# Six inverse roots spread over the partitions by a row in DRAM, windowed attention in another order, and the first loads in smaller pieces

## The chip, the cores and the metric

The kernel runs as one program on one core of one Trainium2 chip. Its engines are TensorE (PE, matrix products into PSUM), VectorE (DVE), ScalarE (ACT), GpSimd (POOL) and SyncE (SP, which issues the DMAs here). Each engine works through its own instructions in program order and waits for the others by semaphores. The metric is the device time of one execution in microseconds (us), the median of three runs.

## The reference

Two blocks over 512 tokens of width 1024, in fp32, one after the other. Cut to the shape of the work (`h` is a normed input, every `@` a product with a weight matrix from DRAM):

```python
def first_block(x, p, ...):
    q, k, v, z_a, b, c, u, z_c = split(rms_norm(x, g) @ w_in, 8)      # 512 columns each
    attn = diff_attention(q, k, v, lam, slopes)                        # 4 heads, two softmaxes each, causal by chunks
    attn = rms_norm(attn, subln_gain, 1e-5) * (1 - lambda_init) * silu(z_a)
    conv = b * causal_conv3(c * u) * silu(z_c)
    x = x + rms_norm(concat(attn, conv) @ w_out, g)
    e = rms_norm(p @ w_ple_proj, g)
    return x + sigmoid(x @ w_ple_gate) * e

def second_block(h, ...):
    u, v, z = split(rms_norm(h, g) @ a_w_in, 3)                        # 2048 columns each
    s = causal_spatial_mix(layer_norm(gelu(v)), w_s, b_s)              # within 128 tokens
    h = h + rms_norm((gelu(u) * s * silu(z)) @ a_w_out, g)
    k, v = split(rms_norm(h, g) @ w_kv, 2)
    q, z = split(rms_norm(h, g) @ b_w_in, 2)
    o = sliding_window_attention(q, k, v, sinks)                       # 16 heads, 4 key heads, window 128
    return h + rms_norm((o * silu(z)) @ b_w_out, g)
```

An `rms_norm` multiplies by `(mean(x^2) + eps)^-0.5` for each token. The kernel does the product with the weight matrix on the un-normed input and multiplies by this inverse root behind it, so that the product need not wait for the norm.

## The kernel before

**Tiles.** Activations lie feature by feature: a tile holds 128 features by 512 tokens. Each fp32 operand is split in two fp32r parts, high and low, and a product is three matmuls (high by high, high by low, low by high). Weights stream from DRAM in tiles `raw` of 128x1024 (512 KB), three in flight. ACT copies a half of one to the high part `whi`, DVE subtracts to get the low part `wlo` (`wsplit`); `wload` issues the DMAs on SP. A `raw` buffer is free once the second `wlo` has read it, and only then the next `raw` can be issued.

**Stages, in the order of time.** `w_in` (6 to 212 us) with the four heads of the first attention between its matmuls; `w_out` (to 255), `w_ple` (to 268) and the gate (to 313); `a_w_in` with the spatial mix (to 593); `a_w_out` (to 682); keys and values (to 706); `b_w_in` (to 831) with the windowed attention between its matmuls, the last of it between those of `b_w_out` (to 886); then the last norm and the output.

**Order.** Every part of the work outside the big products is a generator. A planner (`Flow`) keeps a modelled clock of each engine and resumes a generator when the modelled time of what it waits for has come on TensorE's clock, or, at `yield n`, n modelled ns later. So the program's order on all engines is fixed by these modelled times; `PACE_H`, `H_START` and the like are such delays. The engines themselves know nothing of it and just wait for what is late.

**Norms.** A norm's per-token sums (`st`, eight narrow matmuls) give `var` on DVE and `rstd = var^-0.5` on POOL, as a tile of 128 tokens x 4. To multiply features by it, each partition needs the same row of 512 tokens, the tile `n1rb` (norm n1, of the input), `anrb` (one for each head of the first attention) or `n4rb` (the norm ahead of `a_w_in`). `bcast_wide` makes it for these six and for two others: DVE splits `rstd` into `rh` and `rl`, POOL writes two 128x512 tiles `dgh` and `dgl` with these on the diagonals, and TensorE multiplies both by a matrix of ones (two `bc` matmuls). ACT copies the sum out of PSUM. Each helper records its operations under its own line: `tt` L211, `act` L202, `stt` L207, `ts` L220, `ptt` L215, `dma` L239, `mm` L244, `transpose` L254.

**Names.** First attention: `sc` scores, `s` weights (DVE combines two softmaxes by `rs`, the inverse sums), `tr` their transposes on PE, `pth`/`ptl` their parts, `pv` the product with v, `at` the normed head (DVE, L207). `ev`, `za`: products of `w_in` columns with `n1rb` on DVE. Spatial mix: `rs` at PE are row sums of the masked `w_s`, issued at the end of `spatial_weights`. Windowed attention: a unit is (pair of key heads, query block, which of the two heads), 16 in all; `swa_master` starts them in the order of `ORDER_B`. A unit makes scores `bsc`, weights `be`, transposes `btr`, their parts `bph`/`bpl`, and `bpv`; when both units of a (pair, block) are done, DVE makes `y`, ACT `ybh` and DVE `ybl`, the parts that `b_w_out` reads. `b_w_out` takes blocks 0 and 1 of both pairs first, then blocks 2 and 3. `h_tokens` transposes the residual (`ht`, four transposes a time, eight times) for the last sum.

Of the kernel before, what the change touches and what calls it, by code (L numbers as in the profile page):

```python
# [10 lines left out]
F32 = mybir.dt.float32  # L11
# [6 lines left out]
P = 128  # L18
# [19 lines left out]
ORDER_B = tuple((pr, b) for pr in range(2) for b in range(4))  # L38
AHEAD_END = 1
H_START = 8000  # L40
LAM_AT = 40000
WIDE = ('an', 'n1', 'n3', 'n4', 'n6')
LAT = 130.0
KLATE = 3
BANKS = 7

PACE_A, PACE_B, PACE_LN, PACE_H = 4500, 3500, 8000, 4000
# [106 lines left out]
def block(ctx: ExitStack, tc: tile.TileContext, xT, pT, w_in, w_out, w_ple, w_gate, a_w_in, a_w_out,  # L154
# [7 lines left out]
    whl = ctx.enter_context(tc.tile_pool(name="whl", bufs=WHL))  # L162
    small = ctx.enter_context(tc.tile_pool(name="small", bufs=6))
# [96 lines left out]
    def wsplit(n):  # L260
        raw = raws.pop(n)
        t0 = F.t
        if n in KEPT:
            his, los = [[rt("wk", F32R) for _ in range(2)] for _ in range(2)]
        else:
            hi = whl.tile([P, 1024], F32R, tag="hi", name=nm("whi"))
            lo = whl.tile([P, 1024], F32R, tag="lo", name=nm("wlo"))
            his, los = [[w[:, :512], w[:, 512:]] for w in (hi, lo)]
        for c in range(2):
            r = raw[:, c * 512:(c + 1) * 512]  # L270
            act(his[c], r, AF.Copy, after=t0)
            yield [his[c]]
            if wpos[3] < n:
                yield lambda: wpos[3] >= n
            tt(los[c], r, his[c].bitcast(F32), ALU.subtract, after=t0)

        def part(a, n):

            return his[a // 512][:, a % 512:a % 512 + n], los[a // 512][:, a % 512:a % 512 + n]

        hls[n] = part
        wpos[3] = n + 1
        wload(wpos[2] - 1)

    def wload(cur):
        while wpos[0] < min(len(SEQ), cur + AHEAD_RAW + 1) and wpos[3] >= wpos[0] - WRAW + 1:
# [3 lines left out]
            if wpos[0] < 3:  # L290

                for k in range(2):
                    c = slice(k * 512, k * 512 + 512)
                    dma(nc.sync, raw[:, c], drams[name][i][:, c])
                    dma(nc.sync, x[2 * wpos[0] + k], xT[2 * wpos[0] + k])
# [155 lines left out]

    def norm(stat, d, name, n=1024, eps=EPS, copy=True, half=None):
# [7 lines left out]
        yield [r]  # L460
        if name in WIDE:
# [63 lines left out]
    for k in range(KD):  # L525
# [6 lines left out]
        act(hi, x[k], AF.Copy, scale=v1(V_PRE, k))  # L532
# [169 lines left out]
    def attn_pv(h):  # L702
# [14 lines left out]
        if "an" in WIDE:  # L717
            os = []
            yield from bcast_wide(r, os)
            bc = os[0]  # L720
        else:
            bc = bcast(r)
        rb = rt("anrb")
        act(rb, bc, AF.Copy)
# [222 lines left out]
    def spatial_weights():  # L947
# [18 lines left out]
        yield 4000  # L966
# [410 lines left out]
```

## Time and profile before

| | us |
|---|---|
| median of 3 runs | 894.42 (894.36 to 894.44) |
| profiled execution | 894.61 |
| its span, first to last instruction | 892.9 |
| TensorE busy in the span | 882.8 (99%) |
| VectorE busy | 637.9 (71%) |
| ScalarE busy | 443.4 (50%) |
| GpSimd busy | 77.8 (9%) |
| mean granted clock of TensorE | 0.999 |

The profiled execution stands 0.2 us above the median, and 1.7 us of it lie outside the span. A busy TensorE is not always at its peak: its matmuls are pipelined, and a row's duration is longer than the distance to the next row's start. What a matmul takes of the time is read from the starts of two rows, and a wait from how far a start lies behind the one that the row ahead would allow.

### The profile page before, as it was taken

How to read it: one execution, taken by the hardware profiler on the slowest of the kernel's cores; microseconds unless marked ns; L12 is line 12 of the kernel's file. 1: busy time of each engine (PE TensorE's matmuls, PEld its weight loads, DVE VectorE, ACT ScalarE, POOL GpSimd, SP SyncE). 2: the span in 40 equal slices, each digit the busy share in tenths (PEclk: the TensorE clock that was granted, in tenths of full speed). 3: DMA queues.
4: the chain of work that ended last, by engine and by line, in shares of the span. 5: the costliest groups of instructions: out<-in, count | busy, mean ns of one | idle time of the engine just before them, and what ended most of it. 6: DMA issues, size and time to landing. Idle time of an engine off the chain costs nothing.

```text
span 892.9 us, 12066 instructions
## 1 busy us (share of the span) xinstructions
PE 882.8 (99%) x4348; PEld 744.2 (83%) x4348; DVE 637.9 (71%) x1364; ACT 443.4 (50%) x954; POOL 77.8 (9%) x93
## 2 busy tenths in 40 slices
PE   9999999999999999999999999999999999999997
PEld 7888888888888888888888888888899988887785
DVE  6799989653558893338897766683347876989974
ACT  7455554322556544335443333322344646999763
POOL 0100032100000001001000000000000011434100
PEclk9999999999999999999999999999999999999999
DMA  7231222225423242232232222214232158211353
GB/s 263 94 118 48 71 72 71 95 94 189 142 72 116 73 135 104 99 104 81 73 106 88 89 95 95 95 48 141 94 119 72 71 138 223 65 48 48 120 187 118
DMA packets 30443, 93.20 MB, mean 104 GB/s; under 512 B 3888, under 2 KB 4272, under 8 KB 30384
## 3 DMA queue, kind: packets, MB, share of 16 engines
q1 hardware_dynamic: 30384, 92.44, 30.8%
q8 instruction: 34, 0.56, 0.2%
q14 instruction: 25, 0.20, 0.1%
HBM read 85.60 MB, written 2.10 MB: 98 GB/s over the span
## 4 chain that ended last, share of the span: by engine, by line
PE 87%; DVE 9%; issue 1%; ACT 1%; DMA 1%; SPq 0%; DVEq 0%; ACTq 0%
PE a_w_in L244 29%; PE w_in L244 17%; PE a_w_out L244 10%; PE b_w_in L244 6%; PE w_gate L244 5%; PE w_out L244 5%; PE b_w_out L244 4%; PE kv L244 3%; PE sp L244 2%; DVE wlo L211 2%; PE e L244 1%; PE bsc L244 1%; DVE bpl L211 1%; PE sc L244 1%; DVE be L227 1%
## 5 line engine op out<-in xcount | busy, mean ns | idle before, releaser
L211 DVE TENSOR_TENSOR wlo<-raw,whi 128x512 fp32r<-128x512 f32 x280 | 189.1, 701 | 99.4 <-ACT whi L202 95.6
L202 ACT ACTIVATE whi<-raw 128x512 fp32r<-128x512 f32 x280 | 166.4, 623 | 132.5 <-PE a_w_in L244 39.4
L244 PE MATMUL a_w_in<-h2h,whi 128*128 128x512 f32 x256 | 99.8, 390 | 0.0
L244 PE MATMUL a_w_in<-h2l,whi 128*128 128x512 f32 x256 | 99.7, 390 | 0.0
L244 PE MATMUL a_w_in<-h2h,wlo 128*128 128x512 f32 x256 | 99.6, 389 | 0.0
L244 PE MATMUL w_in<-h1h,whi 128*128 128x512 f32 x224 | 89.3, 401 | 0.4 <-ACT h1h L202 0.4
L244 PE MATMUL w_in<-h1h,wlo 128*128 128x512 f32 x224 | 87.0, 390 | 0.0
L244 PE MATMUL w_in<-h1l,whi 128*128 128x512 f32 x224 | 86.9, 390 | 0.0
L215 POOL TENSOR_TENSOR rstd<-var,mhalf 128x4 f32<-128x4 f32 (+2 forms) x15 | 14.7, 981 | 592.9 <-DVE var L222 536.8
L244 PEld LDWEIGHTS a_w_in<-h2h,wlo 128*128 128x128 f32 x256 | 48.1, 188 | 10.2
L244 PEld LDWEIGHTS a_w_in<-h2h,whi 128*128 128x128 f32 x256 | 48.1, 188 | 9.6
L244 PEld LDWEIGHTS a_w_in<-h2l,whi 128*128 128x128 f32 x256 | 48.1, 188 | 9.4
L211 DVE TENSOR_TENSOR sq<-sq,sq 128x512 f32<-128x512 f32 (+1 forms) x44 | 29.3, 666 | 35.5 <-ACT sq L202 33.6
L244 PE MATMUL b_w_in<-hbh,whi 128*128 128x512 f32 x128 | 52.0, 406 | 0.1
L244 PE MATMUL b_w_in<-hbh,wlo 128*128 128x512 f32 x128 | 50.1, 391 | 0.0
L244 PE MATMUL b_w_in<-hbl,whi 128*128 128x512 f32 x128 | 50.0, 391 | 0.0
L244 PE MATMUL a_w_in<-whi,h2h 128*128 128x512 f32 x128 | 50.0, 391 | 0.0
L244 PE MATMUL a_w_in<-whi,h2l 128*128 128x512 f32 x128 | 49.8, 389 | 0.0
L244 PE MATMUL a_w_in<-wlo,h2h 128*128 128x512 f32 x128 | 49.8, 389 | 0.0
L244 PEld LDWEIGHTS w_in<-h1h,whi 128*128 128x128 f32 x224 | 42.4, 190 | 8.8 <-ACT h1h L202 0.7
L244 PEld LDWEIGHTS w_in<-h1h,wlo 128*128 128x128 f32 x224 | 42.0, 188 | 9.0
L244 PEld LDWEIGHTS w_in<-h1l,whi 128*128 128x128 f32 x224 | 42.2, 188 | 7.9
(269 smaller groups left out, 2034.6 us busy)
## 6 DMA issues: line engine op xcount, KB each, us to landing
raw<-in_a_w_in SPq DMA_DIRECT2D x48, 512.0 KB, 3.2
raw<-in_w_in SPq DMA_DIRECT2D x29, 512.0 KB, 3.2
raw<-in_a_w_out SPq DMA_DIRECT2D x16, 512.0 KB, 3.2
raw<-in_b_w_in SPq DMA_DIRECT2D x16, 512.0 KB, 3.8
raw<-in_b_w_out SPq DMA_DIRECT2D x16, 512.0 KB, 3.6
raw<-in_w_out SPq DMA_DIRECT2D x8, 512.0 KB, 3.3
raw<-in_w_gate SPq DMA_DIRECT2D x8, 512.0 KB, 3.2
x<-in_xT SPq DMA_DIRECT2D x8, 256.0 KB, 5.5
```

Of the source, the lines that this page charges most:

```text
L202: nc.scalar.activation(o, a, func, bias=bias, scale=scale, accum_out=accum_out)
L211: nc.vector.tensor_tensor(o, a, b, op)
L215: nc.gpsimd.tensor_tensor(o, a, b, op)
L227: nc.vector.tensor_tensor_reduce(o, a, b, 1.0, s0, ALU.add, ALU.max, mx)
L244: nc.tensor.matmul(o, a, b, start=start, stop=stop)
```

## The change

1. **Six norms by DRAM.** For `n1`, `n4` and the four `an`, `bcast_wide` and the ACT copy are replaced by `bcast_dma`: SP writes `rstd` (128 x 4) to a row of 4 x 128 in DRAM, and then reads the row back into all 128 partitions (128x512, 256 KB). The two other wide norms stay.
2. **Order of the windowed attention**: blocks 0 and 1 (and 2) of the second pair are started ahead of block 3 of the first; `ht` starts sooner and a little closer together.
3. **First loads**: the first 512 columns of the first weight tile come in two pieces, with the first tile of x between them; ACT makes the first `whi` in two pieces; the first `h1h` is made half by ACT, half by DVE.
4. **Spatial row sums**: 8000 modelled ns behind their operands in place of 4000.

```diff
-ORDER_B = tuple((pr, b) for pr in range(2) for b in range(4))
+ORDER_B = ((0, 0), (0, 1), (0, 2), (1, 0), (1, 1), (0, 3), (1, 2), (1, 3))
-H_START = 8000
+H_START = 0
+DMA_ROW = 2600
-PACE_A, PACE_B, PACE_LN, PACE_H = 4500, 3500, 8000, 4000
+PACE_A, PACE_B, PACE_LN, PACE_H = 4500, 3500, 8000, 3500
@@ wsplit
-            act(his[c], r, AF.Copy, after=t0)
+            if n == c == 0:
+                act(his[c][:, :256], r[:, :256], AF.Copy, after=t0)
+                yield [his[c]]
+                act(his[c][:, 256:], r[:, 256:], AF.Copy, after=t0)
+            else:
+                act(his[c], r, AF.Copy, after=t0)
@@ wload
+                    if wpos[0] == k == 0:
+                        dma(nc.sync, raw[:, :256], drams[name][i][:, :256], 128)
+                        dma(nc.sync, x[0], xT[0])
+                        dma(nc.sync, raw[:, 256:512], drams[name][i][:, 256:512], 128)
+                        continue
@@ norms
+    def bcast_dma(r, name):
+        row_ = dram.tile([NT, P], F32, tag="row", name=nm("row"))
+        nc.sync.dma_start(row_.rearrange("t p -> p t"), r)
+        F.ready[row_.tensor.name] = F.at([r]) + DMA_ROW
+        yield [row_]
+        rb = rt(name + "rb")
+        nc.sync.dma_start(rb, row_.rearrange("t p -> (t p)").unsqueeze(0).to_broadcast([P, T]))
+        F.ready[rb.tensor.name] = F.at([row_]) + DMA_ROW
+        return rb
@@ norm
+        if name in ('n1', 'n4', ''):
+            d[key] = yield from bcast_dma(r, name)
+            return
@@ h1 of the first block
-        act(hi, x[k], AF.Copy, scale=v1(V_PRE, k))
+        if k == 0:
+            act(hi[:, :256], x[k][:, :256], AF.Copy, scale=v1(V_PRE, k))
+            ts(hi[:, 256:], x[k][:, 256:], v1(V_PRE, k), None, ALU.mult)
+            next(w, None)
+        else:
+            act(hi, x[k], AF.Copy, scale=v1(V_PRE, k))
@@ attn_pv
-        if "an" in WIDE:
-            os = []
-            yield from bcast_wide(r, os)
-            bc = os[0]
-        else:
-            bc = bcast(r)
-        rb = rt("anrb")
-        act(rb, bc, AF.Copy)
+        rb = yield from bcast_dma(r, "an")
@@ spatial_weights
-        yield 4000
+        yield 8000
```

Three places show how the instructions stand. The first is the norm of the first head, on SP and DVE. SP before, in the stretch of that head, where only weight tiles stand:

```order
L239 DMA raw_929<-in_w_in 128x1024
L239 DMA raw_1051<-in_w_in 128x1024
L239 DMA raw_1176<-in_w_in 128x1024
L239 DMA raw_1222<-in_w_in 128x1024
L239 DMA raw_1302<-in_w_in 128x1024
```

SP now:

```order
L241 DMA raw_940<-in_w_in 128x1024
L241 DMA raw_1037<-in_w_in 128x1024
L467 DMA row_1053<-rstd_991 128x4x1
L471 DMA anrb_1104<-row_1053 128x512
L241 DMA raw_1177<-in_w_in 128x1024
L241 DMA raw_1209<-in_w_in 128x1024
```

The row's write and its read stand between two weight tiles, and both wait in SP's queue. DVE before, at that head (`rh` and `rl` split the inverse root, `s` is a weight tile of another block of queries):

```order
L220 TENSOR_SCALAR neg_1014<-nmx_991 128x2
L235 CAST rh_1018<-rstd_961 128x4
L211 TENSOR_TENSOR rl_1019<-rstd_961,rh_1018 128x4
L231 RECIPROCAL rs_1029<-ssum_921 128x2
L211 TENSOR_TENSOR rs_1029<-rs_1029,nlam 128x1
L220 TENSOR_SCALAR s_963<-s_963,rs_1029 128x384
L207 SCALAR_TENSOR_TENSOR s_963<-s_965,rs_1029,s_963 128x384
```

DVE now, up to the first reader of `anrb` (`at`):

```order
L213 TENSOR_TENSOR wlo_1023<-raw_855,whi_1022 128x512
L233 RECIPROCAL rs_1115<-ssum_1059 128x2
L213 TENSOR_TENSOR rs_1115<-rs_1115,nlam 128x1
L222 TENSOR_SCALAR s_1069<-s_1069,rs_1115 128x128
L209 SCALAR_TENSOR_TENSOR s_1069<-s_1071,rs_1115,s_1069 128x128
L209 SCALAR_TENSOR_TENSOR at_1132<-pv_918,gsub,anrb_1104 128x512
L209 SCALAR_TENSOR_TENSOR zas_1142<-zat_1084,za_1082 128x512
L213 TENSOR_TENSOR at_1132<-at_1132,zas_1093 128x512
```

`rh` and `rl` are gone, and `at` is now the instruction that waits for SP's second DMA. With it stands all that is behind it on DVE.

The second place is TensorE at the end of the windowed attention. Here `ybh_8155`/`ybl_8156` before and `ybh_8127`/`ybl_8128` now are the third and later feature tiles of the first two blocks, which come out of the second pair. Before:

```order
L244 MATMUL b_w_out_8072<-whi_7965,ybh_7667 128x512
L244 MATMUL b_w_out_8072<-wlo_7966,ybh_7667 128x512
L244 MATMUL b_w_out_8072<-whi_7965,ybl_7668 128x512
L244 MATMUL b_w_out_8071<-whi_8073,ybh_8155 128x512
L244 MATMUL b_w_out_8071<-wlo_8074,ybh_8155 128x512
L244 MATMUL b_w_out_8071<-whi_8073,ybl_8156 128x512
L244 MATMUL bpv_8213<-bph_8086,vz_6598 128x512
L244 MATMUL bpv_8213<-bpl_8087,vz_6598 128x512
L244 MATMUL bpv_8213<-bph_8136,vz_6602 128x512
L244 MATMUL bpv_8213<-bpl_8137,vz_6602 128x512
L244 MATMUL b_w_out_8072<-whi_8073,ybh_8191 128x512
```

Now, from the last `bpv` of the whole attention on (the six `b_w_out` rows left out between the two parts read parts `7602`/`7603` and `7609`/`7610` as well):

```order
L246 MATMUL bpv_8144<-bph_8000,vz_6549 128x512
L246 MATMUL bpv_8144<-bpl_8001,vz_6549 128x512
L246 MATMUL bpv_8144<-bph_8058,vz_6553 128x512
L246 MATMUL bpv_8144<-bpl_8059,vz_6553 128x512
L246 MATMUL b_w_out_8069<-whi_7893,ybh_7602 128x512
L246 MATMUL b_w_out_8069<-wlo_7894,ybh_7602 128x512
L246 MATMUL b_w_out_8069<-whi_7893,ybl_7603 128x512
```

and, six rows further on, up to the first reader of the second pair's part:

```order
L246 MATMUL b_w_out_8070<-whi_7893,ybh_7609 128x512
L246 MATMUL b_w_out_8070<-wlo_7894,ybh_7609 128x512
L246 MATMUL b_w_out_8070<-whi_7893,ybl_7610 128x512
L246 MATMUL b_w_out_8069<-whi_8071,ybh_8127 128x512
L246 MATMUL b_w_out_8069<-wlo_8072,ybh_8127 128x512
L246 MATMUL b_w_out_8069<-whi_8071,ybl_8128 128x512
```

Before, further `bpv` stood behind the first readers of the second pair; now all stand ahead, with twelve `b_w_out` matmuls between the last of them and the first reader.

The third is the end of TensorE's program. Before, the last rows are:

```order
L244 MATMUL b_w_out_8539<-wk_8541,ybh_8299 128x512
L244 MATMUL b_w_out_8539<-wk_8543,ybh_8299 128x512
L244 MATMUL b_w_out_8539<-wk_8541,ybl_8300 128x512
L254 MATMUL ht_8618<-ident,y_5759 128x128
L254 MATMUL ht_8618<-ident,y_5833 128x128
L254 MATMUL ht_8618<-ident,y_5907 128x128
L254 MATMUL ht_8618<-ident,y_5981 128x128
```

Now the last four transposes have 45 matmuls behind them:

```order
L246 MATMUL b_w_out_8497<-wlo_8435,ybh_7692 128x512
L246 MATMUL b_w_out_8497<-whi_8434,ybl_7693 128x512
L256 MATMUL ht_8508<-ident,y_5710 128x128
L256 MATMUL ht_8508<-ident,y_5784 128x128
L256 MATMUL ht_8508<-ident,y_5858 128x128
L256 MATMUL ht_8508<-ident,y_5932 128x128
L246 MATMUL b_w_out_8498<-whi_8434,ybh_8097 128x512
L246 MATMUL b_w_out_8498<-wlo_8435,ybh_8097 128x512
```

The last rows are now `b_w_out` matmuls; the number of transposes is the same.

## Rows read from the trace of the kernel before

**Rows 1.** The page: busy time of the engines, and the busiest DMA queue.
```profile
PE 882.8 (99%) x4348; PEld 744.2 (83%) x4348; DVE 637.9 (71%) x1364; ACT 443.4 (50%) x954; POOL 77.8 (9%) x93
...
q1 hardware_dynamic: 30384, 92.44, 30.8%
```

**Rows 2.** Waits of TensorE: engine, line, what for: us, times, longest.
```profile
PE b_w_out L244 <- DVE ybl L211: 0.8, 2, 0.5
```

**Rows 3.** Timeline, TensorE at the start: start us, us, engine, line, operation.
```profile
6.08 1.41 PE L244 MATMUL w_in<-h1h,whi 128*128 128x512 f32 x3 [0.37 <-ACT h1h L202]
```

**Rows 4.** Timeline, TensorE where the wide matmuls for n1 stand.
```profile
30.08 0.39 PE L244 MATMUL bc<-dgh,onesr 128*128 128x512 f32 x1
...
30.54 0.40 PE L244 MATMUL w_in<-h1h,whi 128*128 128x512 f32 x1
```

**Rows 5.** Timeline of n1: SyncE, GpSimd, ScalarE and VectorE, one row each.
```profile
23.14 3.25 SPq L239 DMA_DIRECT2D raw<-in_w_in  x3
...
24.91 1.41 POOL L215 TENSOR_TENSOR rstd<-var,mhalf 128x4 f32<-128x4 f32 x1 [23.62 <-DVE var L222]
...
30.73 0.60 ACT L202 ACTIVATE n1rb<-bc 128x512 f32<-128x512 f32 x1 [0.74 <-PE bc L244]
...
31.36 1.29 DVE L207 SCALAR_TENSOR_TENSOR ev<-w_in,n1rb 128x512 f32<-128x512 f32 x2 [0.65 <-ACT n1rb L202]
```

**Rows 6.** Windows: us, busy (x) of PE, PEld, DVE, ACT, POOL, clock, DMA, GB/s.
```profile
31.36:107.28 75.92, 75.92 (x370) 63.43 (x368) 73.68 (x197) 42.73 (x110) 3.06 (x3) 1.00 0.21 70
107.28:336.00 228.72, 228.37 (x1055) 189.92 (x1054) 161.93 (x307) 106.00 (x216) 22.53 (x19) 1.00 0.31 107
```

**Rows 7.** Timeline, VectorE and GpSimd around the first head's norm.
```profile
59.38 0.15 DVE L231 RECIPROCAL rs<-ssum 128x2 f32<-128x2 f32 x1
...
60.09 0.62 DVE L207 SCALAR_TENSOR_TENSOR s<-s,rs,s 128x384 f32<-128x384 f32 x1
...
90.51 0.16 DVE L235 CAST rh<-rstd 128x4 fp32r<-128x4 f32 x1
...
91.80 1.27 DVE L220 TENSOR_SCALAR s<-s,rs 128x384 f32<-128x384 f32 x1
93.11 0.62 DVE L207 SCALAR_TENSOR_TENSOR s<-s,rs,s 128x384 f32<-128x384 f32 x1
...
98.51 0.69 DVE L211 TENSOR_TENSOR wlo<-raw,whi 128x512 fp32r<-128x512 f32 x1
...
91.82 1.04 POOL L215 TENSOR_TENSOR dgl<-ident,rl 128x512 fp32r<-128x512 f32 x1
```

**Rows 8.** Timeline, TensorE at the transposes that end this stretch.
```profile
107.28 0.40 PE L244 MATMUL w_in<-h1h,wlo 128*128 128x512 f32 x1
108.03 0.44 PE L254 MATMUL tr<-ident,s 128*128 128x128 f32 x2 [0.35 <-DVE s L207]
```

**Rows 9.** DMA issues: line, KB each, median us from issue to landing.
```profile
out<-y SPq DMA_DIRECT2D x8, 256.0 KB, 2.3
...
trit<-in_tri SPq DMA_DIRECT2D x1, 64.0 KB, 3.2
vec<-in_vecs SPq DMA_DIRECT2D x1, 50.5 KB, 1.8
```

**Rows 10.** Timeline, TensorE at the second group of spatial row sums.
```profile
338.02 0.39 PE L244 MATMUL a_w_in<-whi,h2l 128*128 128x512 f32 x1
338.62 0.74 PE L244 MATMUL rs<-ws,onesr 128*128 128x256 f32 x4 [0.22 <-ACT gv L202]
```

**Rows 11.** Timeline, TensorE at the end of the windowed attention.
```profile
844.15 0.39 PE L244 MATMUL b_w_out<-wlo,ybh 128*128 128x512 f32 x1
845.05 0.50 PE L244 MATMUL b_w_out<-whi,ybl 128*128 128x512 f32 x1 [0.51 <-DVE ybl L211]
845.39 0.60 PE L254 MATMUL ht<-ident,y 128*128 128x128 f32 x4
845.75 0.48 PE L244 MATMUL bpv<-bph,vz 128*128 128x512 f32 x1
```

More of the change, by code (lines that the diff above doesn't have):

```diff
@@ L162, in block @@
     whl = ctx.enter_context(tc.tile_pool(name="whl", bufs=WHL))
+    dram = ctx.enter_context(tc.tile_pool(name="dram", bufs=4, space=bass.MemoryType.DRAM))
     small = ctx.enter_context(tc.tile_pool(name="small", bufs=6))
```

## The prediction

> **What bounds the kernel now.** I read the page first: TensorE is busy in 882.8 of the span's 892.9 us, so a change pays only where it takes work from TensorE or a wait away from it [rows 1]. Next, the waits of TensorE: they are few and short, and the longest group of them is 0.8 us for the low parts at `b_w_out` [rows 2]. Then the windows, since an engine that TensorE is about to wait for does not show in the waits. From 31.36 to 107.28 us VectorE is busy 73.68 of 75.92 us, behind that 161.93 of 228.72 [rows 6]. So in the first attention VectorE has no slack, and what is put ahead of it there or taken from it there counts; at the end of this stretch TensorE stands still for it: the transposes could start 0.23 us after the matmul at 107.28, at 107.51, and start at 108.03 [rows 8]. Call this place the gate. A 128x512 matmul takes 0.23 us of TensorE (two from 30.08 to 30.54 [rows 4]).
>
> The sum is made against the profiled execution, 894.61 us, span 892.9 and 1.7 outside it. It stands 0.2 above the median of 894.42, so the predicted time is the median plus the sum.
>
> **The matmuls that go.** Six pairs of `bc` at 0.46 us each [rows 4]. The four of heads two to four and of n4 lie behind the gate, where TensorE is the bound: 4 x 0.46 = 1.84 us gained. The first two, for n1 and the first head, lie ahead of the gate, and what they give is decided there.
>
> **What VectorE gets back ahead of the gate.** At the first head VectorE does `rh`, `rl`, a reciprocal and two small steps from 90.51 to 93.11, 2.60 us. Elsewhere the same steps without `rh` and `rl` take from 59.38 to 60.09, 0.71 us. So 1.89 us go with the diagonals: the 128x384 step took 1.27 us beside GpSimd's `dgl` at 91.82 [rows 7], and GpSimd no longer writes these tiles. If something else held VectorE there, part of the 1.89 stays: bounds 0.32 (`rh` and `rl` alone, 0.16 each) and 1.89. I take the upper, since nothing else of the group differs from that at 59.38.
>
> **What the DRAM row costs ahead of the gate.** Let r be the time from the issue of the row's write to its landing. No row of before shows a DMA of 512 pieces of 4 bytes each. The nearest are 50.5 KB in 1.8 us and 64 KB in 3.2 us, both on 128 partitions [rows 9]. Lower end 1.8. Upper end: 30384 packets took 30.8% of 16 engines' 892.9 us, 145 ns each; 512 pieces over 16 engines are 32 packets each, 4.6 us, with 1.8 for the rest 6.4 [rows 1, 9]. I take 3.2, the value of the small transfer that had others on the queue, as here. For the read I take 2.4 from the 256 KB out at 2.3 [rows 9], and 0.4 from landing to the next issue (an estimate; three issues took 3.25 us from 23.14 on, 1.1 each with their waits for buffers, which bounds it [rows 5]).
>
> *n1.* `rstd` is ready at 24.91 + 1.41 = 26.32, and SP's weight tile ahead of it is out at 26.39 [rows 5]. TensorE starts 0.27 earlier (below), so the row goes out at 26.1 and `n1rb` is there at 26.1 + r + 0.4 + 2.4 = 28.9 + r. Before, VectorE's `ev` started at 31.36, when ScalarE's copy was done (30.73 + 0.60) [rows 5]. Shift of VectorE: D = r - 2.46, at 3.2 us +0.74. VectorE is dense from here to the gate [rows 6], so all of D arrives there. The weight tile behind the read in SP's queue is held up by the trip, but it has to wait for a buffer of VectorE's anyway, so I cost that at nothing; if it came late, the `wlo` steps that read it would add to D.
>
> *First head.* SP puts the row behind a weight tile, which waits until VectorE's `wlo` frees its buffer. From the order, from the step ahead of `rh` (90.5) VectorE has in front of that a `za`, the 0.71 us group, an `s` of 0.62 and the `wlo` of 0.69 [rows 7], with pipelining 2.5 us; the tile's issue adds 0.3. So the row goes out at 93.3 + D and `anrb` is there at 96.1 + r + D. VectorE reaches `at` behind the `wlo` that ended at about 99.1 [rows 7], less 1.89, plus four small steps (0.85, less than 0.71 + 0.62 for the wide ones), at 98.05 + D. `at` now waits W = r - 1.95, at 3.2 us 1.25, and the weight steps and `s` behind it on VectorE wait with it. So each us of r counts twice.
>
> Gate: 108.03 - 1.89 + D + W = 101.73 + 2r, at 3.2 us 108.1 against 108.03 before: +0.1. It can gain at most until TensorE itself is the last to come: 107.51 - 0.92 (two pairs) - 0.27 (start) = 106.32, -1.71, reached at r = 2.3. All that is gained ahead of the gate is given back there at r = 3.2.
>
> Heads two to four: VectorE has slack there (161.93 of 228.72 [rows 6]), and that covers a wait of `at` of the same size; without it, each would add W. n4: VectorE first reads its row 46 of its instructions later, and that covers the trip; SP's weight tile behind it waited for its buffer anyway.
>
> **Start.** The first `w_in` matmul waits 0.37 us for `h1h` [rows 3], and a modelled end overhangs the next start by 0.16 (0.39 against 0.23 [rows 4]). So the halves can gain at most 0.53, and at least nothing. Three matmuls take 1.41 us there [rows 3] where 2 x 0.23 + 0.39 = 0.85 would be full speed [rows 4], so a sooner start means more of them at the slow pace. I take half, 0.27. It lies ahead of the gate and is no term of its own.
>
> **Row sums.** The second group starts at 338.62, 0.60 us after the row ahead of it, 0.23 would do [rows 10]: 0.37, and 0.11 for the restart, as at 845.05 to 845.39, 0.34 for 0.23 [rows 11]. Moved behind seven more triples, it finds its operand ready: -0.5.
>
> **End of the windowed attention.** TensorE waits twice for `ybl` of the second pair: from 844.15 to 845.05, 0.90 for 0.23, is 0.67 lost [rows 11]; the other has 0.3 of the 0.8 idle [rows 2], with the same 0.16 that the model hides 0.46; 0.11 for each restart. Together 1.3. In the order now twelve `b_w_out` matmuls, 2.7 us, stand between the last `bpv` and their reader, where other `bpv` stood. So -1.3. Bounds: both waits go and a few others with them, -2.6; or units that now come last make TensorE wait instead, +1.0 (as long as the longest two waits here).
>
> **Transposes.** The last four `ht` ran behind the last matmul, beside the last norm; now they stand ahead, on TensorE's path: 845.39 to 845.75, 0.36, and 0.09 on the next row (0.48 for 0.39) [rows 11]: +0.45. The end behind them is a chain of the last norm that they didn't hold.
>
> **Sum.** +0.1 - 1.84 - 0.5 - 1.3 + 0.45 = -3.1: **891.3 us**. As a function of r it is -3.1 + 2(r - 3.2), but not under -4.9.
>
> **Rivals.**
> *A, the row is slow and VectorE stands behind it (slower).* From r = 4.75 nothing is gained, from 5.65 the kernel is over 0.2% slower, and 6.4 gives -3.1 + 6.4 = +3.3, 897.7. For it: 512 pieces of 4 bytes, and each us counts twice. Against: they move 2 KB, and 64 KB took 3.2 [rows 9]. The Trainium skill speaks for it, in "DMA: Bandwidth & Descriptors", section "Rules for kernel authors": a strided last dimension becomes one descriptor for each element, and one should rearrange so that it is contiguous. By that rule the write is 512 descriptors, and the sum would be nearer to that of the upper end, 897.7; no row of before shows such a transfer. Chance 0.14, of which 0.09 over the bound.
> *B, the row takes 3.85 to 4.75 us, or the other terms fall short:* 892.6 to 894.4, say 893.5. Chance 0.13.
> *C, the new order of units brings other waits*, of TensorE for `btr` or `bpv` of the last units: +1.0 in place of -1.3 gives 893.6. For it: VectorE and ScalarE are what the last units wait for, and the same work is only reordered. Against: more matmuls stand behind the last `bpv` now. Chance 0.12.
> *D, the row lands in 2.3 us or less*, TensorE is the last at the gate: 889.5, with the waits of the windowed attention all gone 888.2. Chance 0.11.
>
> **How the numbers follow.** The forecast, r from 2.3 to 3.85 with the end of the attention as worked out, has 0.50 and spans 889.5 to 892.6. 0.2% is 1.8 us, about what a measurement of this kernel tells from no change: faster below 892.6, slower above 896.2. Faster: 0.50 + 0.11 + a little of B and C, 0.65. Slower: 0.09. Same: 0.26. The range takes the forecast, D, C, B and the start of A (r = 5.0): 888.4 to 895.0.
>
> **What would show it.** The row's write and the read as DMA rows, with r between 2.3 and 3.85; `ev` at about 32; `at` of the first head with an idle time of about 1.3 us ahead of it; VectorE's 128x384 step at the first head back at about 0.4 us; the gate near 108.1; `bc` matmuls only for the two norms that stay; no wait at the row sums; `b_w_out` without the two waits for `ybl`; eight groups of `ht` ahead of the last matmul. The prediction is wrong if r is above 4.75, if VectorE is not dense up to the gate, or if the last units make TensorE wait.

## The result, and the profile after

| | us |
|---|---|
| before, median of 5 runs beside it | 894.42 |
| changed, median of 5 runs | 919.42 (917.12 to 920.06) |
| ratio | 1.0273, 95% interval 1.0261 to 1.0285 |
| span of the profiled execution | 915.1 (892.9 before) |

The forecast was 891.3, with a range from 888.4 to 895.0. The change makes the kernel 25.0 us slower. The profiled execution took 917.12 us, the shortest of the five, so the trace shows 22.5 us of the loss. On the page of the changed kernel, TensorE's busy time and the granted clock (here in tenths of full speed, 40 slices of the span):

```profile
PE 888.0 (97%) x4336; PEld 746.8 (82%) x4336; DVE 633.1 (69%) x1353; ACT 439.6 (48%) x949; POOL 63.6 (7%) x81
...
PEclk9989988999999999999999999999999999999999
```

TensorE is busy for 97% of the span where it was for 99% [rows 1], and in slices 3, 6 and 7, all within the first attention, the granted clock is below full speed. The starts of the stages say the same: `w_out` starts at 236.8 us (211.7 before), 25.1 later, and from there on the two kernels differ by no more than 3 us of that: `a_w_in` starts 25.1 later, `b_w_in` 24.1, the span ends 22.2 later. So in this execution everything is lost in the stage with the four heads.

What TensorE and VectorE waited for (engine, line, what for: us, times, longest):

```profile
PE sc L246 <- DVE at L209: 6.0, 1, 6.0
PE sc L246 <- DVE kl L213: 5.6, 2, 4.9
PE st L246 <- ACT asq L204: 4.0, 2, 2.6
PE sc L246 <- ACT kh L204: 1.2, 1, 1.2
```

```profile
DVE at L209 <- DMA anrb<-row: 28.9, 4, 8.8
DVE ev L209 <- DMA n1rb<-row: 10.0, 1, 10.0
```

VectorE waits 28.9 us at its four `at` and 10.0 at the first `ev`, and TensorE waits for what stands behind these. The DMA issues (KB each, median us from issue to landing) and the rows of n1 and the first head on SyncE:

```profile
anrb<-row SPq DMA_DIRECT2D x4, 256.0 KB, 4.7
...
n1rb<-row SPq DMA_DIRECT2D x1, 256.0 KB, 3.8
...
row<-rstd SPq DMA_DIRECT2D x6, 2.0 KB, 8.6
```

```profile
26.73 0.39 SPq L467 DMA_DIRECT2D row<-rstd  x1
37.09 0.34 SPq L471 DMA_DIRECT2D n1rb<-row  x1
```

```profile
103.37 0.43 SPq L467 DMA_DIRECT2D row<-rstd  x1
112.92 0.33 SPq L471 DMA_DIRECT2D anrb<-row  x1
```

The write of 2 KB takes 8.6 us in the median (7.5 to 10.3), where the prediction took 3.2 and had 6.4 as its upper end [rows 9, 1]. The read waits for it: the row of n1 goes out at 26.73 and its read at 37.09. VectorE's first reader starts at 40.92 instead of 31.36 [rows 5], and `at` of the first head 8.83 us after VectorE got to it:

```profile
40.92 1.29 DVE L209 SCALAR_TENSOR_TENSOR ev<-w_in,n1rb 128x512 f32<-128x512 f32 x2 [9.95 <-DMA n1rb<-row]
```

```profile
117.14 0.75 DVE L209 SCALAR_TENSOR_TENSOR at<-pv,gsub,anrb 128x512 f32<-128x512 f32 x1 [8.83 <-DMA anrb<-row]
```

What it does to TensorE, at the place that the prediction calls the gate [rows 8]:

```profile
111.56 0.40 PE L246 MATMUL w_in<-h1h,wlo 128*128 128x512 f32 x1
117.94 0.69 PE L246 MATMUL sc<-kh,qs 128*128 128x384 f32 x1 [5.99 <-DVE at L209]
...
120.29 0.63 PE L246 MATMUL w_in<-h1h,whi 128*128 128x512 f32 x1
120.72 0.63 PE L246 MATMUL w_in<-h1l,whi 128*128 128x512 f32 x1
...
125.44 0.41 PE L256 MATMUL tr<-ident,s 128*128 128x128 f32 x2
```

The transposes that stood at 108.03 stand at 125.44, 17.4 us later. TensorE does not stand at them, though, but at the scores ahead of them, from 111.8 to 117.94: the profile names `at` as what it waited for. The scores read nothing that `at` writes; what can tie them to it is the PSUM bank of `pv`, whose last reader is `at`. Behind the wait, `w_in` matmuls start 0.43 us apart (120.29, 120.72) instead of 0.23, for some 2.5 us: the granted clock is at its lower level, half, after TensorE had stood for 6 us.

### The profile page after: what moved, and what is told of

The parts are those of the page before. It is cut to its first block, busy times and chain, and to the rows that moved or that the text cites. A ratio compares the mean times of both kernels' runs of the same rounds, so it can differ in the third digit from the quotient of the medians.

```text
span 915.1 us, 12024 instructions
## 1 busy us (share of the span) xinstructions
PE 888.0 (97%) x4336; PEld 746.8 (82%) x4336; DVE 633.1 (69%) x1353; ACT 439.6 (48%) x949; POOL 63.6 (7%) x81
## 4 chain that ended last, share of the span: by engine, by line
PE 76%; DVE 3%; ACT 1%; issue 0%; DVEq 0%; ACTq 0%
PE a_w_in L246 29%; PE a_w_out L246 10%; PE b_w_in L246 8%; PE w_in L246 6%; PE w_gate L246 5%; PE w_out L246 5%; PE b_w_out L246 5%; PE kv L246 3%; PE sp L246 2%; PE e L246 1%; DVE be L229 1%; PE bpv L246 1%; PE btr L256 1%; PE bsc L246 1%; PE st L246 1%; DVE y L213 0%
## 5 line engine op out<-in xcount | busy, mean ns | idle before, releaser
L204 ACT ACTIVATE whi<-raw 128x512 fp32r<-128x512 f32 (+1 forms) x281 | 165.9, 621 | 119.3 <-PE a_w_in L246 38.0
```

The source lines that it names most:

```text
L204: nc.scalar.activation(o, a, func, bias=bias, scale=scale, accum_out=accum_out)
```

## The experiments

**The whole change without the DRAM rows** (rest_wide). All six norms on the diagonals and matmuls again, the rest of the change kept:

```diff
-        if name in ('n1', 'n4', ''):
+        if name in ():
@@ attn_pv
-        rb = yield from bcast_dma(r, "an")
+        os = []
+        yield from bcast_wide(r, os)
+        rb = rt("anrb")
+        act(rb, os[0], AF.Copy)
```

> The changed kernel with all six norms back on the diagonals and the matmuls, everything else of the change kept. Theory (the 512 pieces of 4 bytes are slow, and VectorE waits for them in its order): the whole loss goes, and what stays are the small terms: the row sums -0.5, the windowed attention and the transposes together -1.8 (from the starts of the stages in the changed kernel), the start between 0 and -0.5. 892.0, 891.3 to 893.3. Rival 1 (the new order or the first loads take part in the loss): above 896, with the waits of the first attention still in the list.

Measured: 893.81 us, ratio 0.9989 (0.9979 to 1.0). The loss is gone, and so are the waits of the first attention; rival 1 is out. The gain is smaller than the theory said, about 0.6 us. Waits of TensorE in this kernel:

```profile
PE b_w_out L246 <- DVE ybl L213: 1.0, 1, 1.0
PE bsc L246 <- DMA qh<-ql: 0.9, 1, 0.9
PE w_in L246 <- DVE h1l L209: 0.6, 1, 0.6
...
```

**n4 alone by DRAM on top of that** (rest_n4).

```diff
-        if name in ():
+        if name in ('n4',):
```

> As rest_wide, but with the norm n4 alone by the row in DRAM. Theory: nobody waits for this row for tens of us, so its slow write costs nothing and the two matmuls' 0.46 us go: 0.4 to 0.5 under rest_wide, about 891.5. Rival 2 (the trip holds the weight tiles in SP's queue and starves VectorE): not under rest_wide, by the length of the trip up to 8 us over it.

Measured: 893.79 us, ratio 0.9988 (0.9978 to 0.9997). The row's write takes 10.0 us and its read 5.5 in this run, and nobody waits: a slow trip off the path costs nothing, and SP's queue loses nothing by it (rival 2 is out for this place). In the time, the pair's 0.46 us cannot be told from nothing against rest_wide: the two medians are 0.02 us apart, each about 0.7 us under the kernel before. The traces do show it: from the first `a_w_in` matmul to the first with `h2h` as its first operand it takes 89.00 us here (313.73 to 402.73), 89.49 in rest_wide and 90.05 before.

**n1 alone (only_n1) and the heads alone (only_an), on the kernel before.** With all else as before, `bcast_dma` is called for the one or the other:

```diff
+        if name in ('n1',):
+            d[key] = yield from bcast_dma(r, name)
+            return
```

> The kernel before with the norm n1 alone by the row in DRAM. Theory (VectorE waits in its order for the slow write, and is dense behind it): n1rb comes some 9.5 us later, all of it reaches TensorE at the scores, and TensorE runs at half clock for a while behind its longest wait: +9 to +11, 903.5 to 905.5. Rival 6 (only both places together cost, each alone is hidden): within 3 us of before.

> The kernel before with the four heads' norms alone by the row in DRAM. Theory: VectorE waits 5 to 9 us at each of the four, three of them reach TensorE, four pairs of matmuls and the diagonals' 1.9 us go: +12 to +16, 906.5 to 910.5; together with only_n1 about the 25 us of the whole change. Rival 6: within 3 us of before; the prediction's claim that VectorE's slack covers heads two to four: only the first head costs, +5 to +8.

Measured: 903.42 us (ratio 1.0091, 1.0059 to 1.0122) and 911.62 (1.0181, 1.0146 to 1.0215), +8.9 and +17.1 against the 894.56 beside them. With the -0.65 of rest_wide that is 25.3, the whole loss of 25.0: the places add up, and rival 6 is out. only_n1 lies 0.1 us under the lower edge of what was expected, only_an 1.1 over the upper one. TensorE waits in only_an:

```profile
PE tr L256 <- DVE s L209: 11.3, 3, 7.4
PE st L246 <- ACT asq L204: 2.6, 1, 2.6
```

The transposes wait up to 7.4 us for `s`, the VectorE step behind `at`: the same wait as before [rows 8], but many times as long.

**Heads two to four alone** (heads_2_to_4), on the kernel before:

```diff
-        if "an" in WIDE:
+        if h:
+            rb = yield from bcast_dma(r, "an")
+        else:
             os = []
             yield from bcast_wide(r, os)
-            bc = os[0]
-        else:
-            bc = bcast(r)
-        rb = rt("anrb")
-        act(rb, bc, AF.Copy)
+            rb = rt("anrb")
+            act(rb, os[0], AF.Copy)
```

> The kernel before with the norms of heads two, three and four alone by the row in DRAM, the first head's and all others on the matmuls. The prediction's claim (VectorE has slack there and covers the wait): three pairs of matmuls go, -1.4, about 893. Theory from the traces of the changed kernel and of only_an (what stands behind `at` on VectorE is what TensorE needs next, and a PSUM bank stays taken until `at` has read it): VectorE waits 6 to 10 us each time, two of the three reach TensorE, and TensorE is at half clock for some us behind: +6 to +11, 900.5 to 905.5.

Measured: 904.6 us, ratio 1.0119 (1.0103 to 1.0136), +10.5. The prediction's claim that slack of VectorE covers these three falls. The rows (waits of VectorE, then of TensorE, then windows: us, busy of PE, PEld, DVE, ACT, POOL, clock, DMA, GB/s):

```profile
DVE at L209 <- DMA anrb<-row: 20.4, 3, 8.8
```

```profile
PE st L246 <- ACT asq L204: 4.0, 2, 2.6
```

```profile
120.00:145.00 25.00, 21.87 (x95) 17.77 (x94) 15.18 (x47) 9.49 (x27) 1.38 (x1) 0.86 0.47 62
...
165.00:200.00 35.00, 34.92 (x154) 28.45 (x153) 20.75 (x31) 9.81 (x18) 3.54 (x3) 1.00 0.36 109
```

```profile
180.99 0.75 DVE L209 SCALAR_TENSOR_TENSOR at<-pv,gsub,anrb 128x512 f32<-128x512 f32 x1 [8.77 <-DMA anrb<-row]
```

In the stretch around the second head's wait (120 to 145 us) TensorE is 3.1 us idle and at a clock of 0.86, since what it needs next stands behind `at` in VectorE's order. VectorE's 15.18 busy us of 25 there say nothing of slack, as its wait at `at`, 6.26 us, is part of the rest; in the kernel before it is busy 21.68 of these 25 us. The fourth head's `at` waits longest, 8.77 us, and costs nothing: TensorE is busy for 34.92 of the 35 us around it. So the slack covers one head of the three. The mean of [rows 6] mixes two parts: in the kernel before, VectorE is busy 49.97 of the 57.72 us from 107.28 to 165, and 25.59 of the 47 from there to 212; the second and third `at` fall into the first part here, the fourth into the second.

Not all of the 10.5 us come from the heads. In the profiled execution (905.0) `w_out` starts at 219.5, 7.8 us later than before, and the next stages keep that distance. Another 2.5 are lost within `b_w_in`, where TensorE waits 0.84 and 0.55 us for a DMA of the windowed attention (`qh`; 0.6 in all before) and then has half the clock; whether that follows from the edit was not tested.

**A write that is fast, with everything else as in the changed kernel** (one_piece). The row in DRAM is filled with ones near the start (not shown), and one piece of 16 bytes is written in place of the 512, so that this kernel leaves out the norm's values:

```diff
-        row_ = dram.tile([NT, P], F32, tag="row", name=nm("row"))
-        nc.sync.dma_start(row_.rearrange("t p -> p t"), r)
+        row_ = fills.pop()
+        nc.sync.dma_start(row_[0:1, 0:NT], r[0:1, :])
```

> The changed kernel with another row: the row in DRAM is filled with ones near the start, and in place of the 512 pieces one piece of 16 bytes of rstd is written into it, so the read still waits for rstd and for a write, but the norm's values are not used (the result is another). Theory: r falls to about 2.5; with the read at its measured 3.8 in place of 2.4, the prediction's gate formula gives 109.5 at the gate, 1.5 over before, and with the other terms as measured in rest_wide (-0.65) and four pairs (-1.84) 893.4; 891 to 895. Rival 2 (SP's queue or the 256 KB read cost): over 900.

Measured: 892.59 us, ratio 0.9978 (0.9962 to 0.9993). Rows of VectorE and TensorE:

```profile
34.09 1.29 DVE L209 SCALAR_TENSOR_TENSOR ev<-w_in,n1rb 128x512 f32<-128x512 f32 x2 [3.01 <-DMA n1rb<-row]
```

```profile
101.72 0.75 DVE L209 SCALAR_TENSOR_TENSOR at<-pv,gsub,anrb 128x512 f32<-128x512 f32 x1 [0.97 <-DMA anrb<-row]
```

```profile
109.64 0.44 PE L256 MATMUL tr<-ident,s 128*128 128x128 f32 x2 [0.55 <-DVE s L209]
```

`ev` starts 2.73 us later than before, `at` waits 0.97, and the gate is at 109.64 where the expectation said 109.5. That the two figures agree so well is in part luck: with r at 2.5 at both places the shift at n1 would have been 1.44 and the wait at `at` 1.95. With the measured 2.73 and 0.97 the prediction's formula gives 109.84, 0.2 off. So it holds, and with a fast write the change is 2 us faster than before, inside the forecast's range and 1.3 us over the forecast itself. Rival 2 is out here as well.

**A write of four pieces** (row_in_4). A transposition on TensorE and a copy on ScalarE make a 4 x 128 tile first:

```diff
-        nc.sync.dma_start(row_.rearrange("t p -> p t"), r)
+        o = pst("rt")
+        transpose(o[:NT, :P], r)
+        yield [o]
+        rw = small.tile([NT, P], F32, tag="rw", name=nm("rw"), bufs=2)
+        act(rw, o[:NT, :P], AF.Copy)
+        nc.sync.dma_start(row_, rw)
```

> The changed kernel, but rstd is transposed on TensorE to 4 x 128 and copied by ScalarE first, so that the row is written in 4 pieces of 512 bytes instead of 512 of 4 bytes; the read stays. Theory: the write takes 2 to 3 us instead of 7.5 to 10.3. With the transposition and the copy (about 1 us in the chain, 0.2 us of TensorE each) the gate formula of the prediction gives 891 to 893. Rival 2 (SP's queue is what costs): the queue is as before, so most of the 25 us stays, above 905. Rival 3 (the write is slow because it stands behind a weight tile's transfer): the write still takes over 6 us, and the time stays above 910.

Measured: 905.0 us, ratio 1.0113 (1.0098 to 1.0128): 14 us better than the changed kernel, but 12 over the expectation, and none of the theories had it. The first head's rows on GpSimd, TensorE, ScalarE and SyncE:

```profile
91.36 1.02 POOL L217 TENSOR_TENSOR rstd<-var,mhalf 128x4 f32<-128x4 f32 x1 [64.56 <-DVE var L224]
```

```profile
95.32 0.27 PE L256 MATMUL rt<-ident,rstd 128*4 128x128 f32 x1
```

```profile
99.75 0.25 ACT L204 ACTIVATE rw<-rt 4x128 f32<-4x128 f32 x1
```

```profile
100.02 0.27 SPq L472 DMA_DIRECT2D row<-rw  x1
...
101.24 0.33 SPq L476 DMA_DIRECT2D anrb<-row  x1
```

The read goes out 1.2 us after the write, so the write is fast (rival 3 is out). But `rstd` is there at 92.38, its transposition runs at 95.32, and the copy at 99.75: the two steps stand in TensorE's and ScalarE's orders behind other work, and that took 7.4 us where the expectation had 1. This run changes two things at once, and says of the write only that it can be short.

**The real trip in the planner's model** (planned). 9.0 us for the write and 4.7 for the read in place of 2.6 each, so that the readers are placed later:

```diff
-        F.ready[row_.tensor.name] = F.at([r]) + DMA_ROW
+        F.ready[row_.tensor.name] = max(F.at([r]), F.eng["sp"]) + 9000
-        F.ready[rb.tensor.name] = F.at([row_]) + DMA_ROW
+        F.ready[rb.tensor.name] = F.at([row_]) + 4700
```

> The changed kernel with the trip in the planner's model at what it takes (9.0 us for the write, 4.7 for the read, in place of 2.6 each), so that the readers of the rows are placed later in the engines' orders. Theory: the heads' waits on VectorE go nearly all, the wait at n1 stays, because nothing else is ready for VectorE there: only_n1's loss less 1.84, less 1.9, less 0.65, 899 to 903. Rival 7 (the transfers as such cost, by load on the DMA engines or memory): no better than the changed kernel, 915 or more.

Measured: 904.88 us, ratio 1.0103 (1.0075 to 1.0131). No `at` waits any more, so rival 7 is out: it is the place in the order that costs, not the load. What stays comes from n1, as expected, but is 1.9 us more than the upper edge (VectorE's wait, then TensorE's longest):

```profile
DVE ev L209 <- DMA n1rb<-row: 5.8, 1, 5.8
```

```profile
PE w_in L246 <- DVE wlo L213: 7.8, 1, 7.8
```

The 5.8 us are only the part that VectorE could not fill; behind `ev`, which starts at 43.09, its work is late, and a `wlo` that TensorE needs comes 7.8 us late.

**Why the write is slow** (probe_writes). Small writes that nobody reads, put into the kernel before while `a_w_in` runs, each on a line of its own:

```diff
+        d1 = dram.tile([NT, P], F32, tag="pr1", name="pr1")
+        nc.sync.dma_start(d1.rearrange("t p -> p t"), src[:, :NT])
+        yield 16000
...
+        d6 = dram.tile([NT, P, 16], F32, tag="pr6", name="pr6")
+        nc.sync.dma_start(d6[:, :, 0].rearrange("t p -> p t"), src[:, :NT])
```

> The kernel before, with seven small DMAs put in while a_w_in runs, some 16 us apart, that nobody reads (from issue to landing, us). 1: 128 x 4 to a DRAM row in 512 pieces of 4 bytes, as in the change. 2: the same 2 KB in 128 pieces of 16 bytes. 3: 4 pieces of 512 bytes. 4: 128 pieces of 4 bytes. 5: 256 pieces of 4 bytes. 6: 512 pieces of 4 bytes, each in a 64-byte place of its own. 7: 512 pieces of 4 bytes into SBUF. Theory (each small write to DRAM takes long to be confirmed, some 0.2 us, 32 of them in a row on each of 16 DMA engines): 1: 7 to 10, 2: 3 to 4, 3: 2, 4: 3 to 4, 5: 4.5 to 6, 6: as 1, 7: 2 to 3. Rival 4 (pieces of 4 bytes are slow wherever they go): 7 as 1. Rival 5 (pieces that fall into the same 64 bytes hold each other up): 6 as 3, about 2 to 3. Rival 3 (the queue's own load): 1 under 4 us here, where SP has slack.

Landing of number 1 and of number 6, by the lines of their issues:

```profile
L997 SPq DMA_DIRECT2D pr<-vec x1: 426/426/426, 372.5 to 372.5; - x1
...
DMA to landing us min/median/max: 10.7/10.7/10.7
```

```profile
L1012 SPq DMA_DIRECT2D pr<-vec x1: 427/427/427, 453.9 to 453.9; - x1
...
DMA to landing us min/median/max: 3.4/3.4/3.4
```

512 pieces of 4 bytes take 10.7 us side by side and 3.4 with 64 bytes from one to the next. Number 2 (128 pieces of 16 bytes) took 3.8, number 4 (128 of 4 bytes) 9.2, number 7 (512 of 4 bytes, into SBUF) 3.2; for 3 and 5 the profile gives no landing. Number 1's 10.7 us, at a place where SP has slack, rules out rival 3 here too. So neither the theory (so much for each small write) nor rival 4 holds, both by number 6; the pieces hold one another up where they lie close together in DRAM. Number 7 says less than it seems to: its pieces lie 16 bytes apart in SBUF, and at that distance a write to DRAM took 4.2 us (below).

The distance between the pieces (probe_spacing), at 512 and at 16 of them (`c` is the distance in elements of 4 bytes):

```diff
+        def sp(k, c, n=NT, p=P):
+            d = dram.tile([n, p, c], F32, tag=f"pr{k}", name=f"pr{k}")
+            return d[:, :, 0].rearrange("t p -> p t")
+        nc.sync.dma_start(sp(2, 2), src[:, :NT])
+        yield 16000
...
+        nc.sync.dma_start(sp(6, 1, 1, 16), src[:16, :1])
```

> The kernel before with eight small writes to DRAM while a_w_in runs, that nobody reads: rstd-like tiles of 128 x 4 in 512 pieces of 4 bytes, with 4, 8, 16, 32 and 64 bytes from one piece's place to the next (1 to 5), then 16 pieces of 4 bytes from 16 partitions, side by side (6) and 64 bytes apart (7), and 1 again (8). From issue to landing, us. The theory that each small write is slow by itself fell in probe_writes (64 bytes apart took 3.4, side by side 10.7). Theory now (pieces that share a line of memory wait for one another, some 0.4 us each): 1: 9 to 12, 2: 5 to 7, 3: 3.5 to 5, 4: 3 to 3.7, 5: 3.2 to 3.6, 6: 6 to 9, 7: 2 to 3, 8: as 1. Rival 8 (what counts is how many lines or how many pieces in all): 6 as 7, both 2 to 3, and 2 to 4 fall little.

| pieces of 4 bytes | distance, bytes | landing, us |
|---|---|---|
| 512 | 4 | 10.1, again 8.6 |
| 512 | 8 | 5.9 |
| 512 | 16 | 4.2 |
| 512 | 32 | 3.4 |
| 512 | 64 | 4.7 |
| 16 | 4 | 3.1 |
| 16 | 64 | 3.2 |

The fall with the distance is as expected (the 4.7 at 64 bytes, against 3.4 in the run before, is a single measurement, and so is each other figure but the first). But 16 pieces in one stretch of 64 bytes don't hold each other up, against the theory.

How many lie side by side, in four rows or in one (probe_regions; `p` pieces in each of `n` rows of 512 bytes):

```diff
+        def rg(k, p, n):
+            d = dram.tile([n, P], F32, tag=f"pr{k}", name=f"pr{k}")
+            return d[:, :p].rearrange("t p -> p t")
+        nc.sync.dma_start(rg(1, 16, NT), src[:16, :NT])
+        yield 16000
...
+        nc.sync.dma_start(rg(6, 64, 1), src[:64, :1])
```

> The kernel before with seven small writes to DRAM while a_w_in runs, that nobody reads, all in pieces of 4 bytes that stand side by side: 16, 32, 64 and 128 pieces in each of four rows that begin 512 bytes apart (1 to 4, 64 to 512 pieces in all), then 32, 64 and 128 pieces in one row (5 to 7). From issue to landing, us. probe_spacing spoke against a line of 64 bytes, since 16 pieces in one took 3.1. Theory now (what counts is how many pieces fall into the same 512 bytes, some 2.9 us and 0.055 for each of them): 1: 3.8, 2: 4.5, 3: 6.4, 4: 9 to 11, 5: 4.5, 6: 6.4, 7: 9 to 10. Rival 9 (the number of pieces that stand side by side in all): 1 as 6 (64 pieces), 2 as 7 (128 pieces), with 3 and 4 over these. Rival 10 (lines of 64 bytes): 1 to 7 all 7 or more.

```profile
L1008 SPq DMA_DIRECT2D pr<-vec x1: 423/423/423, 372.7 to 372.7; - x1
...
DMA to landing us min/median/max: 3.1/3.1/3.1
```

```profile
L1018 SPq DMA_DIRECT2D pr<-vec x1: 481/481/481, 454.1 to 454.1; - x1
...
DMA to landing us min/median/max: 8.7/8.7/8.7
```

64 pieces as four groups of 16 (rows 512 bytes apart) take 3.1 us, and 64 in one row 8.7. That rules out rival 9 (the number in all) and rival 10 (lines of 64 bytes). The others: four rows of 32, 64 and 128 pieces 5.8, 7.2 and 9.8; one row of 32 and 128 pieces 7.0 and 8.6. So the time goes by how many pieces fall near each other, within a few hundred bytes, or by how many source partitions they come from: the pieces in a row and the partitions are the same number in all seven, and no run tells the two apart. That nearness is part of it is shown by the distances above, all five with 128 partitions. The size that was expected (0.055 us for each piece in 512 bytes) is off by up to 2.5 us for one row of 32 or 64, and how wide such a stretch is stays open, as does what in the memory makes them wait.

During the slow write of n1 in the changed kernel the DMA engines stand still (windows: us, busy of PE, PEld, DVE, ACT, POOL, clock, DMA share, GB/s):

```profile
31.00:32.00 1.00, 1.00 (x6) 0.84 (x5) 0.00 (x0) 0.00 (x0) 0.00 (x0) 1.00 0.15 8
32.00:34.00 2.00, 2.00 (x11) 1.65 (x10) 0.00 (x0) 0.00 (x0) 0.00 (x0) 1.00 0.00 0
34.00:36.00 2.00, 2.00 (x11) 1.65 (x10) 0.00 (x0) 0.00 (x0) 0.00 (x0) 1.00 0.00 0
```

The engines show no packets from 32 us on, and the write lands at 37.0. At the first head the packets end by 106.3, 2.9 us after the issue at 103.37, and the write lands at 112.9. So a packet's mean time, 145 ns by [rows 1], said little on it: half of the time at n1, and two thirds at the first head, lie between the last packet and its confirmation.

**The new order of the windowed attention alone** (order_only). Three constants of the change on the kernel before:

```diff
-ORDER_B = tuple((pr, b) for pr in range(2) for b in range(4))
+ORDER_B = ((0, 0), (0, 1), (0, 2), (1, 0), (1, 1), (0, 3), (1, 2), (1, 3))
-H_START = 8000
+H_START = 0
-PACE_A, PACE_B, PACE_LN, PACE_H = 4500, 3500, 8000, 4000
+PACE_A, PACE_B, PACE_LN, PACE_H = 4500, 3500, 8000, 3500
```

> The kernel before with the new order of the windowed attention and the earlier transposes alone. The prediction's term: -1.3 + 0.45, 893.6; its bounds -2.2 and +1.5. From the stages of rest_wide: 0 to -0.5, 894 to 894.4. One of the two waits for ybl goes, the other is there (1.0 us in rest_wide); the eighth group of transposes stands ahead of the last matmul.

Measured: 894.45 us, ratio 1.0003 (0.9993 to 1.0012): no difference. In its profile the last `b_w_out` matmul starts at 884.68, where it stood at 886.18 before, 1.5 us earlier. Of that 0.7 is there already where `b_w_in` starts (705.15 against 705.87), ahead of all that the edit orders anew; the 0.8 behind it is the size of the term (0.85). The span, however, ends only 0.6 earlier. The rest is in the last output, which lands 3.8 us after SyncE's last issue there and 2.9 us before. That time differs from one execution to the next (2.5 in the changed kernel), so a microsecond of TensorE's at this end is not told from it.

## Why the prediction was wrong

**The first step that failed is r, the write of the row.** The prediction had it between 1.8 and 6.4 us and took 3.2; it takes 7.5 to 10.3. The upper end was worked out from a mean packet time, as if the write's time were that of its packets. It isn't: at n1 all packets, those of the weight tiles among them, show in the 5 us behind the issue at 26.73, and the write of pieces that lie side by side in DRAM is confirmed another 5 us later. No row of before showed a DMA of that kind, as the prediction said, and then the range should not have ended at a figure made from DMAs of another kind. Rival A named the mechanism, its place and its price, 2 us for each us of r; it got 0.14. The Trainium skill's rule that stood beside it ("DMA: Bandwidth & Descriptors", section "Rules for kernel authors", a strided last dimension is one descriptor for each element) was the right warning against this change, but the number of descriptors is not what costs: 512 pieces took 3.4 and 4.7 us 64 bytes apart. The same page, section "Why small descriptors are slow (HBM only)", says that transfers from SBUF to SBUF don't suffer from small descriptors; the 3.2 us into SBUF do not speak against it, but the pieces lay 16 bytes apart there, and at that distance DRAM took 4.2.

**The gate formula was right.** With the measured values, `n1rb` 9.6 us late (40.92 against 31.36) and 8.8 at `at`, it gives 108.03 - 1.89 + 9.6 + 8.8 = 124.5. VectorE's `s` ahead of the transposes starts at 124.53 where it started at 107.48, 17.05 later against 16.5 by the formula; TensorE itself came 0.4 us later still and did not wait for it any more (125.44). In one_piece the formula gives 109.84 with the measured values, and 109.64 was measured. Of its parts, the return of the 1.89 us is right: VectorE's 128x384 step at the first head takes 0.41 us in the changed kernel, at 101.29, where it took 1.27 [rows 7]. The read was taken at 2.4 and takes 3.8 at n1 and 4.2 at the first head (4.7 in the median of the four): another 1.4 and 1.8 us.

**The second step that failed is the cover for heads two to four.** The prediction let VectorE's mean slack behind the gate (161.93 busy of 228.72 us [rows 6]) hide their waits. With 17.4 at the gate and 25.1 at the start of `w_out`, they make up the other 7.7 of the changed kernel; in heads_2_to_4, on their own, 7.8 at the same place. A wait in an engine's order holds up what stands right behind it, and a mean over 229 us says nothing about that: in heads_2_to_4 the slack covered the fourth head's wait, in a stretch that VectorE filled to 54% before, and not the two in the stretch that it filled to 87%. The price named for the case that the cover is gone, W for each, would have been too high: 20.4 us of waits cost 7.8, and 9.2 with the three pairs of matmuls that went.

**The two steps make up the loss of the profiled execution.** With 17.4 at the gate in place of 0.1, and 7.7 behind it in place of the three pairs' -1.38, the prediction's sum is 17.4 + 7.7 - 0.46 - 0.5 - 0.85 = +23.3, 917.7; it took 917.12.

**TensorE's clock was no term**, and is part of the loss: behind its three longest waits (6.0, 4.9 and 2.6 us) the matmuls run at half the clock for a while. From 120.29 to 122.85 six matmuls take 2.56 us, 1.38 at full speed; ahead of 156.96, behind the wait of 2.57 us, ten more start 0.43 to 0.57 us apart (granted clock 0.50).

**n4 costs nothing**, as forecast, and its pair of matmuls gives 0.49 us from start to start (89.49 to 89.00), where 0.46 was forecast. **SP's queue**: TensorE and VectorE have no wait for a weight tile, and the longest of ScalarE's is 2.6 us where it was 3.0; what stood behind the trips cost nothing, as forecast.

**Row sums**: the second group no longer waits (rows at 366.99 and 368.16, neither with idle time ahead of it), and the wait of [rows 10] is gone, as forecast; by the starts above (90.05 to 89.49) that gives 0.56 us, where 0.5 was forecast.

```profile
366.99 0.64 PE L246 MATMUL rs<-ws,onesr 128*128 128x256 f32 x4
...
368.16 0.64 PE L246 MATMUL rs<-ws,onesr 128*128 128x256 f32 x4
```

**The end of the windowed attention**: TensorE gains 0.8 us in order_only, transposes included, where -1.3 and +0.45 were forecast; but not by the step that was named, so that the size fits is luck. One wait for `ybl` stays, 1.02 us where the two before it had 0.8 together [rows 2, 11]:

```profile
866.36 0.39 PE L246 MATMUL b_w_out<-wlo,ybh 128*128 128x512 f32 x1
867.76 0.50 PE L246 MATMUL b_w_out<-whi,ybl 128*128 128x512 f32 x1 [1.02 <-DVE ybl L213]
```

1.40 us from start to start instead of 0.23. What went with the order are two waits of TensorE at 814.89 (`btr`, 0.49 us) and 817.30 (`bsc`, 0.15), which the prediction did not count; the rest of the 0.8 was not traced to rows.

**The start**: the first `w_in` matmul starts at 5.36 instead of 6.08 [rows 3]. The thirteenth stands at 9.03 where it stood at 9.39, 0.36 earlier (0.27 forecast), and a wait of 0.28 us for `h1l` behind it brings the next one to 9.70, behind the 9.62 of before.

## What to carry to other kernels

A DMA through DRAM that stands in an engine's order is priced by what stands behind its reader, not by that engine's mean slack over a long stretch; where the engine is dense around the reader, every us counts once for each such trip, and again where it lets TensorE's clock fall. Before a transfer of a new shape replaces a few matmuls, its time from issue to landing has to be measured by itself: a bound from other transfers is none. A trip off the path cost nothing here, though it took 15.5 us (10.0 and 5.5), but then it gives back no more than the work that it replaces, here 0.49 us of 894. A term of that size does not show in the time, but it does in the distance of two starts within the stage.

## What the runs showed of the hardware that was not expected

A write of 512 pieces of 4 bytes to DRAM took 8.6 to 10.7 us side by side, 5.9 at 8 bytes' distance, 4.2 at 16 and 3.4 at 32, and 3.2 into SBUF at 16 bytes' distance. 16 pieces side by side took 3.1, and so did four such groups in rows 512 bytes apart; 64 in one row took 8.7. In the second half of a write of 10.3 us the DMA engines showed no packet. TensorE's granted clock was 0.50 behind its waits of 6.0, 4.9 and 2.6 us in the changed kernel.
